# A decoder layer's expert loop: the branch for the rare tiles moves from place 18 to place 16 of the order

## Chip, core and metric

The kernel runs on one core of a Trainium2 chip. The metric is the device time of one execution in microseconds (us). The engines are named as in the profile: PE multiplies matrices (PEld loads its weights), DVE and ACT work elementwise, POOL (GpSimd) does small vector work, SP issues the weight transfers. A name with a q behind it (PEldq, SPq) is an engine's sequencer.

## What is computed

One layer of a decoder for 256 prompt tokens and 64 sample tokens (320 in all): adaLN, a diagonal state-space branch beside a convolution branch, and then a mixture of experts. Only the experts matter here: every token goes to 2 of 32 experts, each a gated MLP of 2048 to 256 to 2048.

```python
    expert_idx = gsel[:, None] * EXPERTS_PER_GROUP + topi
    combine = jnp.sum(jax.nn.one_hot(expert_idx, N_EXPERTS, dtype=f32) * wts[..., None], axis=1)
    up = jnp.einsum('td,edf->tef', hf, w_up)
    gt = jnp.einsum('td,edf->tef', hf, w_gate)
    act = jax.nn.silu(gt) * up * combine.astype(h.dtype)[..., None]
    y = jnp.einsum('tef,efd->td', act, w_down)
...
    x = _layer_norm(ALPHA * x + g2 * ff, ln2_g, ln2_b)
```

## The kernel before

The experts are sorted by load, rank 0 being the heaviest. `ORDER` lists the ranks in the order in which they are worked; the position in it is called a **place** here. Places 12 to 15 are the light ranks 22 to 25, place 16 is rank 2 (third heaviest), places 17 to 20 are the light ranks 26 to 29, place 21 is rank 3, and place 29, the last that is always worked, is rank 11.

Tokens lie in groups of 32. `ALWAYS` gives every rank a fixed number of groups that are always computed: one group for a light rank, a tile of four groups ("heavy tile") for ranks 1 to 3. A rank that has more tokens than its fixed groups needs further tiles (`RARE`, 27 of them); they are worked in `rare()`, a branch that all five engines take on one count, `tab[192]`. With these inputs the count is 0 and the whole body is jumped over. Inside, a heavy tile's input `xg`, the heavy result `zb` and the rare weights `wx` share one buffer (tag `xg4`, one copy).

An expert's weights are 6 pieces of 1 MB: four with up and gate weights (two transfers of 0.5 MB each), two with down weights. They go into a ring of 11 buffers; SP issues each as soon as the buffer's last reader is done.

One tile goes through these steps, by the names in the trace: copy of its tokens into `xg` (L1609; DVE takes groups 0 and 2, ACT groups 1 and 3), matmuls into `up` (16 for a light tile, 64 for a heavy one; the trace has two records for each), `part` and `sg` on ACT, small matmuls into `pq`, `A` or `a` and `aT` on DVE, matmuls into `pd`, copies into `z` (light) or `zb` (heavy) on ACT.

What comes back to the tokens is a second kind of work, queued as **steps** in `todo`: four light tiles are packed into one `z` and then yield 8 steps, a heavy tile yields 8 steps of its own. For each of four column blocks they hold a gate (matmul `acc<-g2hl,cls`, then DVE L1692), a split into two halves (ACT cast `phi` L1697, DVE `plo` L1698), matmuls `acc<-phi,hot` and `acc<-plo,hot`, and additions into `x1tok` on DVE (L1708, and L1720 once for two blocks). `tick` takes steps out of `todo`: a rank with one fixed tile puts `SA`=4 steps between its `up` matmuls and 2 behind. In front of the branch `tick(99)` takes all that are left. The scheduler that orders each engine's rows moves almost nothing over the branch.

```python
    for n, rk in enumerate(ORDER[:-2]):
        tl = [t for t, x in enumerate(TILES) if x[0] == rk and t not in RARE]
        if n == GRD:
            tick(99)
            rare()
```

Of the kernel before, what the change touches and what calls it, by code (L numbers as in the profile page):

```python
# [152 lines left out]
def build(tc, A, O):  # L153
# [1587 lines left out]
            f += [lambda b=b, b1=b1: add(b, b1)]  # L1741
        return f

    pk, AFF, GRD, NL2 = {}, 4, 18, 21
    FT = 5
    FL = 8
    ZB = 6
# [534 lines left out]
```

## Time and profile before

| | |
|---|---|
| median of 3 runs | 1693.14 us (1692.36 to 1695.34) |
| the profiled execution | 1690.03 us, its span 1688.2 us |
| PE busy | 1483.2 us (88%) |
| DVE busy | 881.6 us (52%) |
| ACT busy | 552.8 us (33%) |
| POOL busy | 248.6 us (15%) |
| instructions | 28087 |

Busy times are shares of the whole span, most of which (up to 1132 us) lies before the experts; what a change in the expert loop is worth is read from the stretches of that loop. The times of the trace are counted from the span's start. Place 16 begins at 1432 us and place 18, with the branch in front of it, at 1487 us.

### The profile page before, as it was taken

How to read it: one execution, taken by the hardware profiler on the slowest of the kernel's cores; microseconds unless marked ns; L12 is line 12 of the kernel's file. 1: busy time of each engine (PE TensorE's matmuls, PEld its weight loads, DVE VectorE, ACT ScalarE, POOL GpSimd, SP SyncE). 2: the span in 40 equal slices, each digit the busy share in tenths (PEclk: the TensorE clock that was granted, in tenths of full speed). 3: DMA queues.
4: the chain of work that ended last, by engine and by line, in shares of the span. 5: the costliest groups of instructions: out<-in, count | busy, mean ns of one | idle time of the engine just before them, and what ended most of it. 6: DMA issues, size and time to landing. Idle time of an engine off the chain costs nothing. (4 is left out here: it accounts for less than half of the span.)

```text
span 1688.2 us, 28087 instructions
## 1 busy us (share of the span) xinstructions
PE 1483.2 (88%) x10731; PEld 1029.6 (61%) x10731; DVE 881.6 (52%) x1724; ACT 552.8 (33%) x960; POOL 248.6 (15%) x419
## 2 busy tenths in 40 slices
PE   4767988998998899949999999989889998969894
PEld 1444877877786777838899988848423332323331
DVE  5744347666744853695455554463531533424365
ACT  1312433342243234333343433331222423232434
POOL 3021312123223322011100000000200000010013
PEclk9887989999999999979999999988979999989997
DMA  9896999789688886637776645465799799999992
GB/s 287 273 340 221 283 276 240 232 222 260 183 251 202 207 235 206 183 126 235 242 255 221 210 136 170 154 231 208 293 406 412 299 412 402 412 365 412 412 410 73
DMA packets 214899, 447.39 MB, mean 265 GB/s; under 512 B 23811, under 2 KB 134067, under 8 KB 206732
## 3 DMA queue, kind: packets, MB, share of 16 engines
q1 hardware_dynamic: 179572, 395.65, 67.5%
q0 software_dynamic: 29168, 43.15, 11.1%
q10 hardware_dynamic: 6016, 6.70, 1.3%
q8 instruction: 87, 1.43, 0.4%
q14 instruction: 56, 0.46, 0.1%
HBM read 425.53 MB, written 21.77 MB: 265 GB/s over the span
## 5 line engine op out<-in xcount | busy, mean ns | idle before, releaser
L556 DVE TENSOR_TENSOR wlo<-raw,whi 128x1024 fp32r<-128x1024 f32 (+1 forms) x196 | 239.5, 1222 | 313.3 <-ACT whi L555 302.7
L555 ACT CAST whi<-raw 128x1024 fp32r<-128x1024 f32 (+1 forms) x196 | 201.9, 1030 | 419.7 <-PE acc L188 244.8
L188 PE MATMUL acc<-h_hi,whi 128*128 128x320 f32 x864 | 275.5, 322 | 14.0 <-ACT whi L555 11.7
L188 PE MATMUL acc<-h_lo,whi 128*128 128x320 f32 x864 | 272.3, 317 | 0.0
L188 PE MATMUL acc<-h_hi,wlo 128*128 128x320 f32 x864 | 259.0, 320 | 7.4 <-DVE wlo L556 7.1
L188 PEld LDWEIGHTS acc<-h_hi,whi 128*128 128x128 f32 x864 | 166.8, 194 | 41.3 <-ACT whi L555 21.3
L188 PE MATMUL up<-ring,xg 128*32 128x512 f32 x1344 | 181.6, 621 | 7.4 <-PEq L2197 6.5
L188 PEld LDWEIGHTS acc<-h_hi,wlo 128*128 128x128 f32 x864 | 161.8, 194 | 27.3 <-DVE wlo L556 13.2
L188 PEld LDWEIGHTS acc<-h_lo,whi 128*128 128x128 f32 x864 | 167.3, 194 | 2.6 <-issue 2.1
L188 PE MATMUL adp<-raw,scT 128*32 128x512 f32 x672 | 117.2, 673 | 31.5 <-DMA raw<-in_w_ada 31.4
L188 PEld LDWEIGHTS up<-ring,xg 128*32 128x32 f32 x1344 | 43.2, 115 | 100.4 <-issue 85.2
L188 PE MATMUL pd<-ring,aT 128*32 128x512 f32 (+1 forms) x688 | 98.2, 679 | 5.9 <-DVE aT L1870 5.9
L1708 DVE TENSOR_TENSOR x1tok<-x1tok,acc 128x512 f32<-128x512 f32 x80 | 51.8, 684 | 62.7 <-PE acc L188 62.4
L1926 ACT COPY z<-pd 32x512 f32<-32x512 f32 (+1 forms) x92 | 53.1, 577 | 89.0 <-PE pd L188 85.3
L188 PE MATMUL acc<-m_hi,whi 128*128 128x320 f32 x256 | 81.4, 319 | 0.0
L188 PE MATMUL acc<-m_lo,whi 128*128 128x320 f32 x256 | 80.0, 314 | 0.0
L188 PE MATMUL acc<-y_hi,whi 128*128 128x320 f32 x256 | 79.0, 311 | 0.0
L188 PE MATMUL acc<-y_lo,whi 128*128 128x320 f32 x256 | 78.6, 309 | 0.0
L188 PE MATMUL acc<-m_hi,wlo 128*128 128x320 f32 x256 | 78.2, 317 | 0.0
L188 PE MATMUL acc<-y_hi,wlo 128*128 128x320 f32 x256 | 74.7, 311 | 0.0
L188 PE MATMUL acc<-vhl,whi 128*128 128x320 f32 x256 | 57.3, 318 | 13.3 <-ACT vhl L914 12.9
L1609 DVE COPY xg<-XS 128x512 f32 x34 | 14.5, 428 | 81.2 <-PE up L188 78.4
(689 smaller groups left out, 2554.6 us busy)
## 6 DMA issues: line engine op xcount, KB each, us to landing
raw<-in_w_ada SPq DMA_DIRECT2D x128, 512.0 KB, 5.4
ring<-in_moe_w_up SPq DMA_DIRECT2D x120, 512.0 KB, 11.3
ring<-in_moe_w_gate SPq DMA_DIRECT2D x120, 512.0 KB, 10.5
ring<-in_moe_w_down SPq DMA_DIRECT2D x60, 1024.0 KB, 11.3
raw<-in_w_in SPq DMA_DIRECT2D x100, 512.0 KB, 4.9
raw<-in_w_ada SPq DMA_DIRECT2D x80, 256.0 KB, 5.5
raw<-in_w_out SPq DMA_DIRECT2D x32, 512.0 KB, 4.5
rawu<-in_w_ada SPq DMA_DIRECT2D x32, 256.0 KB, 5.4
```

The source lines that it names most:

```text
L188: return PE.matmul(out, lhsT=l, rhs=r, start=a, stop=b, skip_group_check=skip)
L555: S.copy(hi[:, :n], raw_ap)
L556: tt(lo[:, :n], raw_ap, hi[:, :n].bitcast(F32), op=OP.subtract)
L1609: state[g % 2] = (V.tensor_copy if g % 2 == 0 else S.copy)(xg[:, :, 32 * g:32 * g + 32], XS[:, :, bass.ds(off, 32)])
L1708: tt(x, x, o, op=OP.add)
L1926: S.copy(zs[q * ng + nb][0][s0:s0 + m_], pd[m_ * q:m_ * q + m_])
```

## The change

`GRD` is the place in front of which the branch stands. It goes from 18 to 16: the branch and the `tick(99)` ahead of it now stand in front of rank 2, and the places 16 and 17 (rank 2 and rank 26), which were worked ahead of the branch, are worked behind it. No work is added or removed.

```diff
-    pk, AFF, GRD, NL2 = {}, 4, 18, 21
+    pk, AFF, GRD, NL2 = {}, 4, 16, 21
```

**PE in front of the branch.** `zb` steps of rank 2 and the down matmuls of place 17 (`pd_13054`) are the last rows ahead of the branch before the change:

```order
L188 MATMUL acc_13089<-g2hl_10368,cls_10788 128x512
L188 MATMUL pq_13009<-ke_10058,A1_0_10776 128x64
...
L188 MATMUL pd_13054<-ring4_10404,aT_13007 32x512 x4
L188 MATMUL pd_13054<-ring2_10402,aT_13007 32x512 x4
...
L188 MATMUL acc_13105<-plo_10793,hot0_10782 128x512
L188 MATMUL acc_13109<-plo_10793,hot0_10782 128x512
L188 MATMUL acc_13100<-plo_10793,hot0_10782 128x512
L2189 TENSOR_LOAD tab_10203
L2197 COMPARE_AND_BRANCH
```

After the change the rows ahead of it are the down matmuls of place 15 (`pd_12695`) and then nothing but the 8 steps of the light pack of places 12 to 15 (24 `phi` and `plo` matmuls; the gates of two blocks stand further up):

```order
L188 MATMUL pd_12695<-ring10_10775,aT_12674 32x512 x4
L188 MATMUL pd_12695<-ring4_10404,aT_12674 32x512 x4
L188 MATMUL acc_12735<-phi_10398,hot0_10782 128x512
L188 MATMUL acc_12739<-phi_10398,hot0_10782 128x512
...
L188 MATMUL acc_12748<-g2hl_10368,cls_10788 128x512
L188 MATMUL acc_12735<-plo_10793,hot0_10782 128x512
...
L188 MATMUL acc_12784<-plo_10793,hot0_10782 128x512
L188 MATMUL acc_12775<-plo_10793,hot0_10782 128x512
L2189 TENSOR_LOAD tab_10203
L2197 COMPARE_AND_BRANCH
```

So the steps that end ahead of the branch are now those of the light pack, with no expert's matmuls among them.

**PE at the heavy tile of rank 2.** Before, its `up` matmuls (`up_12768`) follow place 15's down matmuls at once, with steps of the light pack among them:

```order
L188 MATMUL pd_12695<-ring4_10404,aT_12674 32x512 x4
L188 MATMUL up_12768<-ring2_10402,xg_12727 32x512 x16
L188 MATMUL up_12768<-ring3_10403,xg_12727 32x512 x16
L188 MATMUL acc_12825<-phi_10398,hot0_10782 128x512
L188 MATMUL acc_12825<-plo_10793,hot0_10782 128x512
L188 MATMUL acc_12829<-phi_10398,hot0_10782 128x512
L188 MATMUL acc_12829<-plo_10793,hot0_10782 128x512
L188 MATMUL up_12768<-ring5_10405,xg_12727 32x512 x16
```

After, they (`up_17615`) are the first rows behind the branch, and the light tile of place 17 (`up_17764`) comes between the heavy tile's `pq` and `pd`:

```order
L2197 UNCONDITIONAL_BRANCH x2
L188 MATMUL up_17615<-ring2_10402,xg_17574 32x512 x16
L188 MATMUL up_17615<-ring3_10403,xg_17574 32x512 x16
L188 MATMUL up_17615<-ring5_10405,xg_17574 32x512 x16
L188 MATMUL up_17615<-ring7_10772,xg_17574 32x512 x16
L188 MATMUL acc_17686<-kc_72,clu_10789 128x128
L188 MATMUL acc_17769<-g2hl_10367,cls_10788 128x512
L188 MATMUL acc_17778<-g2hl_10367,cls_10788 128x512
L188 MATMUL pq_17690<-kc_72,a4_17691 128x128 x2
L188 MATMUL up_17764<-ring1_10401,xg_17753 32x512 x4
...
L188 MATMUL pd_17697<-ring8_10773,aT_17681 32x512 x4
```

The steps have left the heavy tile; those of rank 2 itself now lie among the matmuls of places 17 to 19 (before: 16 and 17).

**DVE behind the branch.** Before, the first rows gather tokens for places 20 and 21 (`xg_18049`, `xg_18131`); the inputs of places 18 and 19 were gathered ahead of the branch:

```order
L2197 UNCONDITIONAL_BRANCH x2
L1609 ISA
L1609 COPY xg_18049<-XS_10399 128x512
L1608 TENSOR_LOAD tab_10203
L1608 ISA x2
L1609 ISA
L1609 COPY xg_18131<-XS_10399 128x16x32
```

After, the first two copies are rank 2's own groups 0 and 2 (`xg_17574`), which the first `up` matmuls behind the branch read:

```order
L2197 UNCONDITIONAL_BRANCH x2
L1609 ISA
L1609 COPY xg_17574<-XS_10399 128x16x32
L1608 TENSOR_LOAD tab_10203
L1608 ISA x2
L1609 ISA
L1609 COPY xg_17574<-XS_10399 128x16x32
```

The heavy tile's gather has moved from ahead of its matmuls by many rows to directly in front of them. On SP the branch stands behind the first down piece of place 17 instead of place 19, with the same row (the second down piece) behind it. The body that PE jumps over has 1102 rows between its two branch rows in both kernels.

## Rows read from the trace of the kernel before

**Rows 1.** Windows: stretch, length, busy us (instructions) by engine, PEclk, DMA share, GB/s.
```profile
1336.00:1480.00 144.00, 132.28 (x909) 47.84 (x899) 58.49 (x110) 43.07 (x79) 6.21 (x11) 0.95 1.02 409
...
1480.00:1488.00 8.00, 1.50 (x11) 0.47 (x13) 1.88 (x3) 0.00 (x0) 1.31 (x2) 0.76 0.77 303
1488.00:1496.00 8.00, 7.11 (x58) 2.17 (x49) 2.12 (x6) 2.34 (x5) 3.21 (x8) 0.82 0.71 270
...
1496.00:1646.00 150.00, 135.51 (x1037) 54.23 (x1041) 63.29 (x147) 55.76 (x107) 14.39 (x34) 0.98 1.02 412
```

**Rows 2.** The chain that ended last: shares of the span, then its first pieces.
```profile
PE 8%; DVE 2%; ACT 1%; issue 1%; DMA 0%; POOL 0%; POOLq 0%; DVEq 0%; ACTq 0%
...
1486.67 0.30 issue
1486.97 5.62 PE up L188 x32
```

**Rows 3.** The branch's line, by engine: duration ns min/median/max, first and last start.
```profile
L2197 SPq EVENT_SEMAPHORE  x9: 17/17/17, 1483.1 to 1488.8; - x9
...
L2197 DVEq EVENT_SEMAPHORE  x2: 21/21/21, 1486.5 to 1486.6; - x2
...
L2197 SPq COMPARE_BRANCH  x1: 53/53/53, 1477.8 to 1477.8; - x1
L2197 PEldq COMPARE_BRANCH  x1: 6306/6306/6306, 1480.1 to 1480.1; - x1
```

**Rows 4.** Timeline around the branch: start, us, engine, line, operation, [idle before <-releaser].
```profile
1478.76 0.69 DVE L1698 TENSOR_TENSOR plo<-zb,phi 128x512 fp32r<-128x512 f32 x1
...
1480.04 1.28 DVE L1708 TENSOR_TENSOR x1tok<-x1tok,acc 128x512 f32<-128x512 f32 x2 [0.59 <-PE acc L188]
...
1486.97 5.58 PE L188 MATMUL up<-ring,xg 128*32 128x512 f32 x32 [6.50 <-PEq L2197]
...
1492.62 0.43 DVE L1609 COPY xg<-XS 128x512 f32 x1 [10.69 <-PE up L188]
1493.80 0.47 DVE L1609 COPY xg<-XS 128x512 f32 x1 [0.76 <-DMA ring<-in_moe_w_down]
```

**Rows 5.** Timeline where place 16 begins (PE and DVE).
```profile
1432.30 7.35 PE L188 MATMUL up<-ring,xg 128*32 128x512 f32 x64
...
1435.62 0.69 DVE L1698 TENSOR_TENSOR plo<-z,phi 128x512 fp32r<-128x512 f32 x1 [0.56 <-ACT phi L1697]
```

**Rows 6.** Groups by form, 1432 to 1516 us: a gate's product on DVE.
```profile
L1692 DVE TENSOR_TENSOR z<-z,acc 128x512 f32<-128x512 f32 x4 | 2.7, 687 | 7.5 <-ACT z L1926 4.6 <-PE acc L188 2.9
```

**Rows 7.** Windows of 2 us: the clock behind the branch.
```profile
1490.00:1492.00 2.00, 2.00 (x20) 0.50 (x12) 0.00 (x0) 0.25 (x1) 0.43 (x2) 0.77 0.84 270
```

**Rows 8.** Timeline of PE in places 16 and 17, step by step.
```profile
1465.10 1.92 PE L188 MATMUL pd<-ring,aT 128*32 128x512 f32 x16
1466.84 1.04 PE L188 MATMUL up<-ring,xg 128*32 128x512 f32 x8
1467.81 0.49 PE L188 MATMUL acc<-g2hl,cls 64*128 64x512 f32 x1
1468.23 0.96 PE L188 MATMUL acc<-phi,hot 128*128 128x512 f32 x3
1469.03 0.86 PE L188 MATMUL acc<-plo,hot 128*128 128x512 f32 x3
```

**Rows 9.** Timeline of PE behind the branch: place 18's down matmuls, place 21's first `up`.
```profile
1495.97 1.92 PE L188 MATMUL pd<-ring,aT 128*32 128x512 f32 x16 [0.32 <-DVE aT L1870]
...
1515.52 1.04 PE L188 MATMUL up<-ring,xg 128*32 128x512 f32 x8
```

**Rows 10.** Timeline of SP: the fourth up piece of place 19.
```profile
1476.26 0.33 SPq L1492 DMA_DIRECT2D ring<-in_moe_w_up  x1
```

**Rows 11.** Timeline of PE at the end: the last place's `up` and down matmuls.
```profile
1654.52 1.04 PE L188 MATMUL up<-ring,xg 128*32 128x512 f32 x8
...
1669.18 3.21 PE L188 MATMUL pd<-ring,aT 128*32 128x512 f32 x16
```

## The prediction

> **What bounds the kernel now.** The windows come first: through the whole expert loop the weight stream moves 409 to 412 GB/s, but for a stand around the branch, and PE is busy 132 of 144 us ahead of it and 135 of 150 us behind it [rows 1]. Both are near their limit, so the windows alone don't say which one counts. The chain that ended last does: followed back from the end it reaches PE as it comes out of the branch at 1486.67, and its next piece is place 18's `up` [rows 2]. A weight transfer that was late would stand in that chain; DMA has 0% of the span in it, and that is an output. At the end the stream stops at about 1646, while the last place's `up` begins at 1654.5 and its down matmuls at 1669.2 [rows 1, 11]: 9 to 23 us of spare. So the end is PE's, with the small operations of DVE and ACT between its groups, and what counts is when PE gets to a fixed point behind the branch. I take the start of place 18's down matmuls, 1495.97 now [rows 9]. What is behind it is the same work in both kernels but for half of place 19's `up`, which the change draws forward; place 19 then waits for ACT's `z` copies behind place 18's down matmuls anyway, so I count nothing for it. Work up to 1432.30, where place 16 begins [rows 5], is the same too.
>
> So the question is what the stretch from 1432.30 to 1495.97, 63.7 us, becomes. The work in it is the same: heavy tile of rank 2, light tiles 17 and 18, 8 steps of the light pack, 8 steps of rank 2, one branch. Only the order differs, and with it what can hide what.
>
> **First part: the light pack's steps, alone.** Ahead of the branch they have no matmuls of an expert beside them any more, and DVE sets their pace. They begin as before: the first `plo` ends at 1435.62 + 0.69 = 1436.3 [rows 5]. Up to the end of the last `plo` DVE then does 3 pairs of additions (1.28 each), 1 single one (a half of that, 0.64), 3 more `plo` (0.69) and 2 gates (0.69) [rows 4, 6]: 3.84 + 0.64 + 2.07 + 1.37 = 7.9 us. A pair waits 0.59 behind its `plo` for PE [rows 4]; a gate lies in that gap twice, once it stays open. The last `plo` ends at 1436.3 + 7.9 + 0.6 = 1444.8; I take 1445 (1444 to 1447, the upper end if additions wait for a free PSUM buffer). In the kernel before, PE did the heavy tile's matmuls in this time.
>
> **Second part: the branch and the gather.** Now the last `plo` ends at 1479.45 and PE starts again at 1486.97, 7.5 us later, 6.3 of them in the jump itself [rows 3, 4]. The skipped body has the same length, so I take the same price: 1452.5. Before the change the tile behind the branch had its input already. Now DVE has to copy two of rank 2's four groups first; it is back at 1486.6, 0.4 ahead of PE, its copies follow each other by 1.18 and the second takes 0.47 [rows 3, 4], and a register load comes ahead of the first (0.2 estimated). That is 1.85 − 0.4 = 1.5 behind PE: 1454.0. ACT's two copies are earlier, since it reaches the branch with its last cast. Bounds: 0 if the register is there and the copies follow closely, 3 if each waits for a load of its own.
>
> **Third part: the heavy `up`, its first 4 us at the lower clock.** 128 records at 7.35 per 64 [rows 5] are 14.7 us. [...] The pause is about as long after the change (8 us instead of 6.5), so 1.9 more: the `up` ends at 1470.6. Bounds: 0 to 1.9 for the clock.
>
> **Fourth part: from there to place 18's down matmuls.** By the new order PE does 88 records of light `up` (11 groups of 8 at 0.97), 5 groups of 16 down records (about 1.8; 1.74 in the row), 24 step matmuls (8 threes at 0.80, and 0.8 more as some stand single), 4 gates at 0.42 [rows 8], and two small class matmuls, the wait for their cast and five `pq` groups: eight small things at the 0.42 of a single small matmul in the same rows, an estimate of 3.4. 10.7 + 9.0 + 7.2 + 1.7 + 3.4 = 32.0. Start of place 18's down matmuls: 1470.6 + 32.0 = 1502.6. Bounds: 29 if every group runs at its best rate, 35 if DVE's additions hold up PSUM buffers.
>
> **Sum.** 1502.6 − 1496.0 = +6.6 us. The profiled execution took 1690.03 (its span is 1688.2, and 1.8 lies around it), so 1696.6; it was 3.1 below the median of the runs shown, 1693.14, and on that basis I predict 1699.7, rounded to 1700. What is lost: before, the light pack's steps lay under the heavy tile, and rank 2's under place 17 with a tail in front of the branch. Now 12.7 us of steps stand alone (1432.3 to 1445), and the gather is bare. What is won, rank 2's steps filling gaps in places 17 and 18, is less.
>
> **What covers the weights.** The stream will stand longer, and I cost that at nothing. Place 19's fourth up piece goes out when place 17's first down buffer is free: at 1476.26 now [rows 10], after the change about 22 us into the fourth part (all but 10 us of its groups stand ahead), 1492.6. Now the stream dries up at 1480 + 8 × 303/412 = 1485.9 and starts again at 1496 − 8 × 270/412 = 1490.8 [rows 1], a stand of 4.9. So that piece flowed from 1480.8 on (two pieces of 1 MB, 2.55 us each at 412 GB/s, ahead of 1485.9); after the change it flows at 1494.6 (2.0 behind its issue, as from SP's last event at 1488.8 to 1490.8 [rows 1, 3]), 13.8 later, and as the stand of 4.9 does not follow, the stream is 8.9 late. Place 21's first piece is the eighth behind the restart, there at 1490.8 + 8 × 2.55 = 1511.2 for a use at 1515.52 [rows 9]: 4.3 spare. PE itself is 6.6 late, so 2.3 of it is used up, and it holds. Were there no spare at all, the end would be 8.9 late, 2.3 more than forecast. SP's own pause (1477.8 to 1488.8 [rows 3]) lies ahead of the first buffer that the heavy tile frees (about 1460), and costs nothing.
>
> **Rivals.**
> The stream takes over: if its stand is larger than I count, or the spare at place 21 smaller, the end shifts by up to 9 to 11: 1702 to 1704. For it: a heavy tile frees a buffer each 3.6 us, slower than 2.55. Against it: the spare above. Chance 0.10.
> No change: the gather is hidden, the clock does not fall, and the groups run at their best rates; −1.5, −1.9 and −3 off +6.6 leave +0.2, two of them +1.7 to +3.2: about 1693 to 1696. Chance 0.15.
> A cheap branch: the jump takes under 0.2 us at its new place instead of 6.3. That leaves +0.5, or 1693.6. Against it: the same 1102 rows are jumped over, and SP too shows 5.3 us from its jump to its next row (1477.8 to 1483.1) [rows 3]. Chance 0.06. [...]
> Faster: rank 2's steps fill the bubbles of places 17 to 20 entirely. The tail of rank 2's steps and the branch leave PE without work for much of 1480 to 1488 now (1.5 us busy [rows 1]), and behind the change nothing of rank 2 is left in front of a branch. If its steps then cost PE nothing (9 us of the fourth part) and the class and `pq` groups lie in gaps that I count twice (1.2), the fourth part is 21.8 and the sum −3.6, or 1689.5. It decides from a fourth part of 22.0 down. Against it: step matmuls are PE's own time, and its groups' best rates give no less than 29. Chance 0.07.
> The forecast, +3.5 to +11 with PE as the bound: 0.62.
>
> **Numbers.** About 0.2% (3.4 us) is what a measurement of this kernel can tell from no change. Slower holds the forecast and the stream, 0.72; same holds "no change" and the cheap branch, 0.21; faster 0.07. The range has to leave out 2 in 10: its lower end, 1694, takes in most of "no change" and leaves out faster and a part of the cheap branch; the upper, 1705, holds +12: the upper bounds (2 for the first part, 1.5 for the second, 3 for the fourth) on top of the forecast make +13, and not all come together; the stream's case is in it too.
>
> **What would show it.** In the changed trace: no `up` between 1432 and 1452, DVE busy nearly throughout; the branch on PE at about 1446, 6.3 long; the first `up` at about 1454, behind L1609 copies and at the lower clock; place 18's down matmuls near 1503; a weight stream that stands twice or more between 1455 and 1495, 13 to 14 us in all; and a chain that still starts at the branch with no weights in it. The forecast is wrong if PE waits for weights at places 17 to 21, if the jump is short, or if the down matmuls of place 18 come before 1499.

## The result and the profile after

The changed kernel takes 1704.0 us (median of 10 runs), the kernel before 1695.4 (10 runs, the three shown above among them). The ratio is 1.0057, its 95% interval 1.0033 to 1.0081: 9.7 us slower, 5.6 to 13.7. The sign is as predicted, the size is not: +6.6 was forecast. 1704.0 lies in the range given (1694 to 1705), but by luck: the upper end was added up from other bounds than the one that failed, and the kernel before came out 2.3 us above the median that the forecast started from.

The two profiled executions, 1690.03 and 1709.85, differ by more than that, and 8.3 us of it has nothing to do with the change: place 15's down matmuls begin at 1429.16 before and at 1437.42 after, with the same work ahead of them. Over the twelve profiles of this study that point lies anywhere from 1428.4 to 1439.9. So stretches are compared here, counted from the start of place 15's down matmuls ("from place 15"): to place 18's down matmuls, to place 21's first `up`, and from there to the end of the span.

| us | before | after |
|---|---|---|
| from place 15 to place 18's down matmuls | 66.8 | 77.5 |
| from place 15 to place 21's `up` | 86.4 | 98.7 |
| from place 21's `up` to the end | 172.7 | 172.0 |

The rows that they start from, place 15's down matmuls, before and after (start, us, engine, line, operation, idle before and releaser):

```profile
1429.16 3.38 PE L188 MATMUL pd<-ring,aT 128*32 128x512 f32 x16 [0.32 <-DVE aT L1870]
```

```profile
1437.42 3.46 PE L188 MATMUL pd<-ring,aT 128*32 128x512 f32 x16 [0.32 <-DVE aT L1870]
```

Each stretch is of one profile. The last one, the same work in all twelve, lies between 171.4 and 173.9, so a difference of 1 or 2 us between two profiles says little; the timing's 9.7 us (5.6 to 13.7) is the better size of the loss, and 12.4 is what there is to explain in these two profiles.

The loss of 12.4 us is complete at place 21's `up`; behind it almost nothing is lost or won back, which fits PE setting the end. It has two sides to be looked at: when the heavy `up` starts, and what it costs to get there.

The windows of the changed kernel around the branch (stretch, length, busy us and instructions of PE, PEld, DVE, ACT, POOL, then the granted clock, DMA share, GB/s), beside [rows 1]:

```profile
1440.00:1448.00 8.00, 4.77 (x16) 2.45 (x9) 3.55 (x6) 3.54 (x6) 0.00 (x0) 0.71 1.04 416
1448.00:1456.00 8.00, 6.48 (x18) 3.31 (x17) 6.15 (x10) 1.24 (x2) 0.00 (x0) 0.82 1.01 408
1456.00:1464.00 8.00, 0.77 (x3) 0.29 (x2) 1.88 (x3) 0.00 (x0) 1.18 (x2) 0.60 1.01 400
1464.00:1472.00 8.00, 3.47 (x20) 1.52 (x24) 1.71 (x4) 1.24 (x2) 2.55 (x6) 0.54 0.11 41
```

PE does next to nothing for 12 us, from 1456 to 1468, where it lost 6.5 before. While the steps run (1440 to 1456) DVE has 9.7 us of work in 16, and the clock granted to PE is 0.50 of full speed from 1444 to 1450 and 0.80 in 1450 to 1452 by windows of 2 us. And the stream still runs at 400 GB/s up to 1464.

The branch's line in the changed kernel, by engine (duration ns min/median/max, first and last start), beside [rows 3]:

```profile
L2197 SPq EVENT_SEMAPHORE  x9: 17/17/17, 1460.3 to 1467.8; - x9
...
L2197 PEldq EVENT_SEMAPHORE  x2: 51/51/51, 1462.6 to 1462.7; - x2
L2197 DVEq EVENT_SEMAPHORE  x2: 21/21/21, 1462.8 to 1462.9; - x2
...
L2197 SPq COMPARE_BRANCH  x1: 53/53/53, 1455.0 to 1455.0; - x1
L2197 PEldq COMPARE_BRANCH  x1: 6126/6126/6126, 1456.4 to 1456.4; - x1
```

PE is out of its jump at 1462.5 and DVE at 1462.8, 6.8 and 7.0 us behind the end of the last `plo` (forecast until PE starts again: 7.5). But SP gives its last sign at 1467.8, 12.8 us behind its own branch row. The timeline of the changed kernel shows who waits for that:

```profile
1443.99 0.69 DVE L1698 TENSOR_TENSOR plo<-z,phi 128x512 fp32r<-128x512 f32 x1 [0.56 <-ACT phi L1697]
1444.10 1.62 PE L188 MATMUL acc<-phi,hot 128*128 128x512 f32 x3 [3.23 <-ACT phi L1697]
...
1446.48 0.69 DVE L1692 TENSOR_TENSOR z<-z,acc 128x512 f32<-128x512 f32 x1 [1.80 <-PE acc L188]
...
1454.57 0.33 SPq L1495 DMA_DIRECT2D ring<-in_moe_w_down  x1
1455.07 0.69 DVE L1698 TENSOR_TENSOR plo<-z,phi 128x512 fp32r<-128x512 f32 x1
...
1467.91 1.29 ACT L1609 COPY xg<-XS 128x512 f32 x2 [13.93 <-SPq L2197]
1468.00 0.43 DVE L1609 COPY xg<-XS 128x512 f32 x1 [9.77 <-SPq L2197]
```

ACT and DVE both copy the heavy tile's input 0.1 to 0.2 us behind SP's last sign, and PE's `up` follows. PE's own timeline carries the rest of the sum, beside [rows 5, 9]:

```profile
1468.53 15.64 PE L188 MATMUL up<-ring,xg 128*32 128x512 f32 x128 [11.76 <-ACT xg L1609]
...
1514.95 1.92 PE L188 MATMUL pd<-ring,aT 128*32 128x512 f32 x16
1522.25 3.47 PE L188 MATMUL pd<-ring,aT 128*32 128x512 f32 x16 [0.32 <-DVE aT L1870]
1532.74 3.58 PE L188 MATMUL pd<-ring,aT 128*32 128x512 f32 x16 [0.32 <-DVE aT L1870]
1536.15 13.92 PE L188 MATMUL up<-ring,xg 128*32 128x512 f32 x128
```

### The profile page after: what moved, and what is told of

Same layout as the page of the kernel before. It is cut to its first block, busy times and chain, and to the rows that moved or that the text cites. A ratio compares the mean times of both kernels' runs of the same rounds, so it can differ in the third digit from the quotient of the medians.

```text
span 1708.1 us, 28076 instructions
## 1 busy us (share of the span) xinstructions
PE 1487.2 (87%) x10731; PEld 1036.3 (61%) x10731; DVE 881.9 (52%) x1724; ACT 551.9 (32%) x960; POOL 246.4 (14%) x419
## 5 line engine op out<-in xcount | busy, mean ns | idle before, releaser
L188 PE MATMUL up<-ring,xg 128*32 128x512 f32 x1344 | 177.2, 609 | 12.8 <-ACT xg L1609 11.8
L188 PE MATMUL acc<-phi,hot 128*128 128x512 f32 (+1 forms) x136 | 49.0, 458 | 7.3 <-ACT phi L1697 7.1
```

The source lines that it names most:

```text
L188: return PE.matmul(out, lhsT=l, rhs=r, start=a, stop=b, skip_group_check=skip)
```

## The experiments

Theory A, formed from these rows: `xg` of the heavy tile shares its one buffer (tag `xg4`) with the rare weights `wx`, which SP's transfers fill inside the branch. So the copy behind the branch may not write before SP has crossed it, and the price of the place is SP's: its arrival at the branch plus 12.8 us. Theory B is the prediction's: PE's jump and DVE's return set it, and what is over comes from the drained steps. (The expectation of the first run below has another theory B, that the engines' own fetch of code or registers holds up the copies.) All kernels were timed beside the kernel before.

**POOL fills the rare weights.** SP takes no branch.

```diff
-    def fetch(e, c, w):
+    def fetch(e, c, w, q=None):
...
-        state["sp"] = SY.dma_start(out=w, in_=v[:, c - 4])
+        state["sp"] = (q or SY).dma_start(out=w, in_=v[:, c - 4])
...
-        eng = (PE, V, S, GP, SY)
+        eng = (PE, V, S, GP)
...
-                        return fetch(e, c, pm2.tile([128, D], F32, name="wx", tag="xg4", bufs=1))
+                        return fetch(e, c, pm2.tile([128, D], F32, name="wx", tag="xg4", bufs=1), GP)
```

> The changed kernel, but the rare tiles' weights are fetched by POOL, and SP does not take the branch. Theory A (rank 2's gather waits for SP's late events behind the branch, because its buffer is shared with the rare weights that SP fills): the gather starts when DVE and ACT are back, 7 us behind the last plo, the heavy up 9 us behind it instead of 12.8, place 18's down matmuls 66.5 us behind the first plo's end instead of 70.3, and the time is some 4 us under the changed kernel (1700 where that has 1704). Theory B (the gather is held up by the engines' own fetch of code or registers): the heavy up stays 12.8 us behind the last plo and the time does not move. The weight stream should also stand less, as SP's pause of 13 us is gone; by both theories that alone is worth nothing.

Measured: 1702.0 us, ratio 1.0036 [1.0015, 1.0058], +6.1 us. That alone does not tell it from the changed kernel's 1.0057, but the trace does (the branch's line, then the timeline):

```profile
L2197 PEldq EVENT_SEMAPHORE  x2: 51/51/51, 1458.0 to 1458.1; - x2
L2197 DVEq EVENT_SEMAPHORE  x2: 21/21/21, 1458.7 to 1458.8; - x2
```

```profile
1451.02 0.68 DVE L1698 TENSOR_TENSOR plo<-z,phi 128x512 fp32r<-128x512 f32 x1
...
1458.06 1.29 ACT L1609 COPY xg<-XS 128x512 f32 x2 [8.13 <-PEq L2197]
1459.43 0.43 DVE L1609 COPY xg<-XS 128x512 f32 x1 [5.26 <-DVEq L2197]
...
1459.96 16.28 PE L188 MATMUL up<-ring,xg 128*32 128x512 f32 x128 [7.24 <-DVE xg L1609]
```

The copies now follow PE's and DVE's own signs, and `up` starts at 1459.96, 8.3 us behind the end of the last `plo` (12.8 with SP in the branch). The stretch to place 21's `up` is 94.8, 3.9 shorter. So SP's wait is 3.9 of the 12.4 in these profiles; the other 8.4 (94.8 less 86.4) stay when it is taken away. That the buffer is what ties the copies to SP rests on the kernel's code and on these releasers; `wx` in a buffer of its own was not tried.

**No jump at 16, no jump at 18, no barrier.** The changed kernel without `rare()`, the kernel before without it, and neither `rare()` nor the drain:

```diff
         if n == GRD:
             tick(99)
-            rare()
```

> The changed kernel without the branch and its body (no tile beyond those given to each rank is worked, none is needed for these inputs), the clearing of the steps in front of place 16 kept. Theory A: the 12.8 us from the last plo to the heavy up shrink to 1 or 2 and the up is not cold, so the stretch from the first plo's end to place 18's down matmuls goes from 70.3 to 56 to 59 us, about that of the kernel before (59.7), and the time to about 1691. If the jump were not what costs, it would stay over 65.

> The kernel before without the branch and its body, the clearing of the steps in front of place 18 kept. Theory A: the jump and the cold restart cost 7 to 9 us there, so 1686 to 1688, and the difference to the same edit at place 16 is what the steps cost when they stand alone: 4 to 6 us. If the weights' stream is the bound instead, the time falls by no more than 5, the length of its stand.

> Neither the branch nor the clearing of steps, at any place (again no tile beyond those given to each rank is worked). Theory A: the least that the loop can take, 1 to 4 us under the kernel before without its branch (1684 to 1687), since rank 2's last steps then spread over place 18. If clearing the steps costs nothing, it equals the variants that keep it.

Measured: 0.9960 [0.9937, 0.9983], 0.9973 [0.9950, 0.9997] and 0.9950 [0.9926, 0.9975], or −6.8, −4.6 and −8.5 us, intervals about 4 either way. Place 15's down matmuls and place 21's first `up` without the jump at 16, then without the one at 18:

```profile
1435.61 2.77 PE L188 MATMUL pd<-ring,aT 128*32 128x512 f32 x16 [0.32 <-DVE aT L1870]
...
1517.93 14.18 PE L188 MATMUL up<-ring,xg 128*32 128x512 f32 x128
```

```profile
1431.10 3.31 PE L188 MATMUL pd<-ring,aT 128*32 128x512 f32 x16 [0.32 <-DVE aT L1870]
...
1509.16 14.34 PE L188 MATMUL up<-ring,xg 128*32 128x512 f32 x128
```

From place 15 to place 21's `up` it is 82.3, 78.1 and 78.1 us. By these profiles the branch itself costs 8.3 us at place 18 (86.4 less 78.1) and 16.4 at place 16 (98.7 less 82.3), and the drain costs nothing at 18 and 4.3 at 16 (82.32 less 78.06). In the run at 16 without the jump, the heavy `up` matmuls lie among the steps again: it is the branch that keeps them apart. Of the 12.4 lost, 8.1 is a dearer branch and 4.3 the drain; of the 8.1, 3.9 is SP's wait, and what makes up the other 4.2 (the copies directly ahead of `up`, the slower clock, with 0.50 granted from 1458 to 1470 in the changed kernel and from 1486 to 1490 before) was not taken apart. The timing bears out the first (by the ratios the branch costs 16.4 us at 16 and 4.6 at 18), but not the second: the two kernels without the jump, with the drain at 16 and at 18, take 1689.6 and 1688.8 us, where 4 to 6 apart was expected, so the 4.3 rests on one profile of each. At 18 the timing (−4.6) alone would also allow the rival of that expectation, a stand of the stream of no more than 5; the 8.3 of the profile speaks against it.

**The steps stay behind the branch.** This takes theory B's first part away: PE reaches its branch 1.3 us from place 15 instead of 19.0. What the kept steps add is not what the reference adds, though the branch's body is jumped over (the expectation says otherwise; why was not looked into), so these two kernels serve for their times only; every engine has as many instructions as in the changed kernel.

```diff
         if n == GRD:
-            tick(99)
+            kept = todo[:]
+            todo.clear()
             rare()
+            todo[:0] = kept
```

> The changed kernel, but the light pack's 8 steps are no longer drained ahead of the branch: they are kept and taken up again behind it, among the matmuls of places 16 to 18 (with a rare tile at work the result would be off, since both share buffers; with these inputs none is, and all of the computation is done). PE then reaches its branch right behind place 15's down matmuls, about 15 us earlier. Theory A (the heavy tile's copies share the buffer of the rare weights, and so wait for SP's last sign behind its branch; SP's arrival at its branch is set by the weight stream, not by PE): the first heavy up does not come earlier, it stays some 13 us behind SP's own branch row, 30 us behind the start of place 15's down matmuls, and as the steps' matmuls now lie behind it, the time is that of the changed kernel or up to 8 us more, 1704 to 1712. Theory B (the drained steps of the first part and PE's own jump set it): the first heavy up comes about 20 us earlier, 11 us behind place 15's down matmuls, and the time falls by about 12 us to 1690 to 1694.

> As the kernel before, with the rare weights filled by POOL besides, so that SP takes no branch. Both theories: nothing is left for the gather to wait for but the jump, PE's 6.1 us; the first heavy up comes 9 to 12 us behind the start of place 15's down matmuls. Against the changed kernel the stretch from place 15's down matmuls to place 18's is 12 us shorter or more (77.5 there), 1688 to 1694. If theory A holds, the difference to the run without POOL's filling is 12 to 20 us, if theory B holds it is 0 to 4.

Measured: 1716.3 us with SP in the branch, ratio 1.0103 [1.0072, 1.0134], and 1699.7 with POOL filling, 1.0019 [0.9995, 1.0043]: 16.6 us apart on one chip. The branch's line and the timeline of the first:

```profile
L2197 SPq EVENT_SEMAPHORE  x9: 17/17/17, 1456.3 to 1463.3; - x9
...
L2197 PEldq COMPARE_BRANCH  x1: 6166/6166/6166, 1433.7 to 1433.7; - x1
...
L2197 SPq COMPARE_BRANCH  x1: 53/53/53, 1451.1 to 1451.1; - x1
```

```profile
1432.39 3.53 PE L188 MATMUL pd<-ring,aT 128*32 128x512 f32 x16 [0.32 <-DVE aT L1870]
...
1463.54 0.43 DVE L1609 COPY xg<-XS 128x512 f32 x1 [31.21 <-SPq L2197]
...
1464.07 2.82 PE L188 MATMUL up<-ring,xg 128*32 128x512 f32 x10 [21.62 <-ACT xg L1609]
```

PE is at its branch 17.7 us earlier, and yet `up` starts 31.7 us from place 15 (31.1 in the changed kernel). PE waits 21.6 us for copies that wait for SP, which comes to its branch at 1451.1 all the same, 18.7 us from place 15 (17.6 in the changed kernel). With POOL filling, `up` starts 10.1 us from place 15:

```profile
1434.77 3.54 PE L188 MATMUL pd<-ring,aT 128*32 128x512 f32 x16 [0.32 <-DVE aT L1870]
...
1444.83 12.76 PE L188 MATMUL up<-ring,xg 128*32 128x512 f32 x96
```

So theory B is out as long as SP takes the branch. The first was slower still than theory A's range, 1704 to 1712, probably as the kept steps lie bare behind the wait; its profiled stretch is 26.0 us longer than before and the timing says +17.5 (12.2 to 22.8), a gap that I can't explain. The second missed its range, 1688 to 1694: its stretch is 89.7, not shorter than before. That the steps' matmuls, now behind the branch, are not hidden there is the likely reason, not shown by itself.

**POOL fills at 18.** The control for the same edit on the kernel before.

> The kernel before with the rare weights filled by POOL, SP out of the branch: the control for the same edit at place 16. There the tile behind the branch has its input already, and only the copies of place 21's heavy tile wait for SP's sign. Theory A: nothing for PE hangs on it, the time is that of the kernel before within 3 us, 1692 to 1698. Rival: SP's pause itself (12 us in which no weight is issued) costs time wherever it stands: 3 to 4 us faster, as at place 16.

Measured: 0.9977 [0.9953, 1.0001], −3.9 us (−8.0 to +0.2), no certain gain. The stretch is 85.8 (86.4 before), and PE's `up` is 0.4 behind its own sign in both. I take it as theory A's case: at 18 nothing of PE hangs on SP. The rival is not excluded by the timing. What does move is ACT's copy for place 21's heavy tile: it starts at 1489.07 with PE's sign (1489.0) as its releaser, 0.1 us behind it.

**The branch at 19 and at 20.** First the place alone, then 19 and 20 with POOL filling as above.

```diff
-    pk, AFF, GRD, NL2 = {}, 4, 18, 21
+    pk, AFF, GRD, NL2 = {}, 4, 19, 21
```

> The kernel before with the branch one place later, in front of rank 28: rank 2's steps are through by then, the drain finds nothing, and the next light tile's input is copied ahead of the branch. What the place costs is then the jump alone. If the loss at a place is jump plus bare steps plus bare gather, it is 2 to 4 us faster than the kernel before, whose last two plo and their additions stand bare ahead of the jump: 1691 to 1694. Rival: the stream or the later work has no room for it, no difference.

> The branch in front of rank 28 with the rare weights filled by POOL, so that SP takes no branch. With SP in it at this place PE's second sign behind its jump came at 1497.1, 0.5 us behind SP's first sign and 5.6 behind the end of its own jump, and ACT's cast waited another 3.1 for copies that stood behind SP's last sign. Theory A (SP, 6 us later at its branch than PE, is what PE and ACT waited for): without SP PE's up follows its jump within 1 us, the stretch from place 15's down matmuls to place 21's up falls from 96.5 to 86 to 88 us, and the time is that of the kernel before within 3 us, 1693 to 1699. Rival (place 19's weights had not landed, as the view names a weight transfer): the wait of 5 to 6 us stays, the stretch is 92 or more, and the time is 4 us or more above the kernel before.

> As the kernel before this one, one place later, in front of rank 29: no steps are left at all ahead of the branch, and only the copies of rank 3's heavy tile stand behind it, a place ahead of their use. Theory (a place costs the jump of 6.1 us, the slower clock behind it, and what stands bare around it): 7 to 9 us above the kernels without a branch, so the stretch from place 15's down matmuls to place 21's up is 85 to 88 us, and the time is that of the kernel before within 3 us; a place that hides the jump itself does not exist, since PE's own sequencer takes it. Rival: the pause at 20 hides behind the weight stream, which catches up: 4 us faster or more.

Measured: 1.0045 [1.0017, 1.0074] at 19, slower and not faster, a miss; 1.0028 [1.0004, 1.0053] with POOL filling; 1.0004 [0.9982, 1.0027] at 20. With POOL filling at 19 the time is 1700.2 us, above what theory A gave (1693 to 1699). The stretches are 96.5, 89.2 and 88.1. At 19 with SP in the branch, by the branch's line and the timeline of PE and ACT:

```profile
L2197 SPq EVENT_SEMAPHORE  x9: 17/17/17, 1496.6 to 1503.8; - x9
...
L2197 PEldq EVENT_SEMAPHORE  x2: 51/51/51, 1491.5 to 1497.1; - x2
```

```profile
1497.44 4.90 PE L188 MATMUL up<-ring,xg 128*32 128x512 f32 x24 [9.15 <-DMA ring<-in_moe_w_up]
...
1504.21 1.33 ACT L1609 COPY xg<-XS 128x512 f32 x2 [13.50 <-SPq L2197]
...
1505.88 0.79 PE L188 MATMUL acc<-g2hl,cls 64*128 64x512 f32 x2 [3.12 <-ACT cls L1669]
```

PE's second sign is 5.6 us behind its first and 0.5 behind SP's first; later ACT's cast stands behind a copy into `xg4` that waits for SP's last. With SP out of the branch at 19 another engine takes its place:

```profile
L2197 PEldq EVENT_SEMAPHORE  x2: 51/51/51, 1499.0 to 1499.2; - x2
L2197 ACTq EVENT_SEMAPHORE  x2: 17/17/17, 1502.1 to 1502.2; - x2
```

```profile
1502.14 4.92 PE L188 MATMUL up<-ring,xg 128*32 128x512 f32 x24 [5.69 <-ACTq L2197]
```

ACT is last here, since it has place 18's `z` copies to do behind PE's down matmuls before it jumps (at 1496.9, PE at 1492.9), and PE waits 3 us for its sign. So the wait of 5.6 did not go altogether; the stretch of 89.2 lies between what the two theories gave. The rival, weights of place 19 that had not landed, is out all the same: their last `up` transfer is issued 47.5 us from place 15 in both kernels (1476.62 and 1484.77), and with SP out of the branch `up` starts 3.5 us sooner (64.8 instead of 68.3). At 20 the order is the same, ACT's sign last, and the stretch 88.1. No place tried beats 18.

## Why the prediction was right and wrong

**Right: the sign, the bound and the stream.** PE set the end, the chain again starts at the branch, with the heavy `up`. In the changed kernel it starts at 1467.64, with ACT's copy of `xg`; its first long pieces (start, us, what), beside [rows 2]:

```profile
1468.53 15.66 PE up L188 x128
1486.09 3.57 PE up L188 x32
```

The weights stand longer, about 17.5 us by the eight-us windows from 1464 to 1512 (13 to 14 predicted), and the spare at place 21 covered it: in the list of waits from 1430 to 1700 no PE row waits for a weight transfer. The jump is 6.1 us; the cheap branch is out.

**Wrong: the second part, 12.8 us instead of 9.0.** The step that failed is that the gather costs 1.5 us behind PE, 3 at the most, with SP's own pause put at nothing. (The register load in it, 0.2 by estimate, takes 0.30 to 0.32 us in the five `TENSOR_LOAD` rows of L1608 on DVE in the trace before.) It cost 5.3: `up` starts 12.8 us behind the end of the last `plo`, and the sum has 7.5 of that for the jump. I read SP's pause for what it does to the weight stream only. Its signs are also what the copies into a buffer shared with the branch's body waited for, 0.1 to 0.2 us behind the last, and that `xg` and `wx` share one was known. The trace before hints at it; this ACT row of its timeline stands 0.1 us behind SP's last sign at 1488.8 [rows 3], though it names PE as the releaser:

```profile
1488.94 1.31 ACT L1609 COPY xg<-XS 128x512 f32 x2 [9.44 <-PE up L188]
```

The run with POOL filling at 18 bears this reading out: without SP the same copy starts 0.1 us behind PE's sign, where before it was 2.4 behind. At 18 that copy was for place 21, and nothing hurried. At 16 it is for the next matmul, and SP comes to its branch late, because the weight pieces in front of it go out at the stream's pace (400 to 416 GB/s in the windows from 1440 to 1464), the last at 1454.57. The restart is not "last `plo` plus 9.0" but SP's arrival, 17.6 us from place 15, plus 12.8 to its last sign, plus 0.7 for copy and `up`: 31.1, where the prediction has 24.8 (1454.0 less 1429.16). With SP out of the branch at 16 the stretch to place 18's down matmuls (1433.38 to 1507.01) is 73.6 us, 6.8 above the kernel before, which is nearly the forecast's 6.6; that its other errors cancel there, +2.4 of the first part against the rest, is chance, but what the sum lacked in the changed kernel is SP.

**Wrong: the first part, 11.1 instead of 8.7.** DVE alone does not set the pace of the steps. PE drops to its lower clock, 0.50 granted from 1444 to 1450, its triples of step matmuls take 1.62 and 1.65 us where [rows 8] has 0.96, and DVE's gates wait 1.80 and 0.97 for them. In the changed kernel this excess is hidden behind SP's arrival; with POOL filling it is 11.1 too, and shows.

**The rest of the sum.** The third part was 15.6 (16.6), the fourth 30.9 (32.0), both inside their bounds. The third part's 1.9 us for the clock is the 5.58 of 32 records less half of the 7.35 of 64 [rows 4, 5]; no run shows the clock as a frequency, only as a share granted, 0.77 in 1490 to 1492 before [rows 7], and in the changed kernel 0.50 in 1468 to 1470, 0.68 in 1470 to 1472 and 1.00 behind that, where the 128 records took 15.64, 0.9 above twice 7.35. Behind place 18 I counted nothing; 1.65 came on top, with two groups of down matmuls at 3.47 and 3.58 us (2.72 and 1.92 before). Forecast +6.6, then +3.8, +2.4, −1.0, −1.2 and +1.7, and 0.1 ahead of the first `plo`: 12.4.

**The rivals.** "Faster" failed where the prediction said: the fourth part did not fall under 22. "No change" is outside the interval: the gather was bare. "The stream takes over" gave a time close to the one measured, but by a mechanism that did not happen.

The jump is dear in every trace with a branch here, 6046 to 6306 ns on PE; what that time goes into no run shows.

## What to carry to other kernels

A branch that several engines take can hold up an engine that has crossed it, if the next buffer it needs is one that another engine, not yet across, uses in the body (here `xg4` and SP, whose last sign in the changed kernel came 5.3 us behind the end of PE's jump): look up which engine writes that buffer inside, when that engine comes to the branch, and put no first reader or writer of such a buffer directly behind it. An engine that issues transfers may arrive at the pace of the stream: SP came 17.6 and 18.7 us from place 15, though PE was 17.7 us earlier in the second case. Taking it out of the branch (here POOL fills) was worth 16.6 us in that case, 3.9 by the profiles in the changed kernel, and nothing certain at 18, where PE waited for nothing of SP's. Work that is drained in front of a branch should be priced with the clock that PE has there: its mean was 0.71 and 0.82 in the two windows of the steps, and 0.95 over the stretch ahead of the branch in the kernel before [rows 1].

## What the runs showed of the hardware

SP stands twice at its branch: 5.2 to 5.3 us from its jump to its first sign in four traces, and then 5.7 (before, 1483.1 to 1488.8), 7.5 (after), 7.0 and 7.2 us to its last. The other engines have one stand in the changed kernel, 6.1 us on PE (6.0 to 6.3 over all traces with a branch), 5.6 on DVE and 5.2 on ACT; only at 19 did a second sign of PE's come apart from its first, as told above. Why SP's second stand is there and differs was not tried.
